# Softmax over 16,384 rows: a schedule written by hand in a critical section, and the same work as a fixed schedule of the tile framework with passes of eight rows

## The chip, the core and the metric

The kernel runs on one core of a Trainium2 chip. Four engines matter here: VectorE (DVE in the profile), ScalarE (ACT), SyncE (SP), which only issues loads and waits, and the core's 16 DMA engines, which carry data between the chip's memory (HBM) and the core's own memory (SBUF, 128 partitions wide). The metric is the device time of one execution in microseconds (us); lower is better.

## What is computed

The input is 32 x 512 rows of 1024 float32 numbers, 64 MiB in all, and the output has the same size. Each row goes through a softmax at temperature 0.5:

```python
scaled = x / temperature
shifted = scaled - np.max(scaled, axis=-1, keepdims=True)
exp_x = np.exp(shifted)
return exp_x / np.sum(exp_x, axis=-1, keepdims=True)
```

Every number is read from HBM once and written once, so 134.2 MB pass through the DMA engines.

## The kernel before

**Tiling.** The 16,384 rows are cut into 16 tiles. A tile has 1024 rows: eight rows in each of the 128 partitions, 4096 KB. A tile is loaded by one DMA and stored by one DMA (`LOADS` and `STORES`). All work is done in place, in a ring in SBUF that has room for 48 rows per partition (`RING`), which is six tiles. A load of tile i therefore has to wait until the store of tile i-6 has landed.

**Passes.** The computing goes in passes of four rows per partition (`GROUP = 4`), two passes to a tile, 32 in all. For pass g there are five steps:

- `maximum(g)` (line 91, VectorE): one reduction finds the largest of each row, for four rows at once.
- `shift(g)` (line 101, VectorE): the maximum times -2 becomes the bias of the exponential.
- `exponential(g)` (line 109, ScalarE): four activations, one for each row, write exp(2x + bias) over the row and sum it up as they go. Each is followed in the profile by a short instruction that reads the accumulator.
- `invert(g)` (line 122, VectorE): the reciprocal of the sums.
- `divide(g)` (line 128, VectorE): four multiplications, one for each row.

**The order of the work.** The whole program stands in one critical section of the framework (`tc.tile_critical()`, line 154), in which the framework inserts nothing: the order on each engine is the order of the code, and every dependence is a semaphore that the code names itself. There are three lists, one for each engine:

- SP issues the 16 loads in order (line 142). From the seventh on it waits for the store that frees the place. After the last load it waits for the remaining stores to land (line 158).
- ScalarE does the exponentials of pass g, and then issues those stores whose last pass is g-1 (`store`, line 149). A store waits for the divisions of its tile. So the store of a tile stands behind four exponentials of the next tile.
- VectorE does maximum and shift of pass g, and then reciprocal and division of pass g-1. So the division of a pass stands behind the maximum of the next pass, and where that pass begins a new tile, behind the wait for that tile's load (line 90).

Loads and stores are issued on two queues, q1 from SP and q10 from ScalarE, and both are served by the same 16 DMA engines. Line 206 of the profile is the end of the framework's context, outside the critical section; it closes every execution.

Of the kernel before, what the change touches and what calls it, by code (L numbers as in the profile page):

```python
# [1 line left out]

# [4 lines left out]

LOADS = [8] * 16  # L10

STORES = [[8]] * 16

RING = 48

GROUP = 4


def _places(loads, ring):
    places, p = [], 0  # L20
    for k in loads:
        if p + k > ring:
            p = 0
        places.append(p)
        p += k
    return places


@with_exitstack
def kernel(  # L30
    ctx: ExitStack,
    tc: tile.TileContext,
    x: bass.AP,
    temperature: bass.AP,
    out: bass.AP,
):
    nc = tc.nc
    f32 = mybir.dt.float32
    scale = 1.0 / float(temperature)
    extreme = mybir.AluOpType.max if scale > 0 else mybir.AluOpType.min  # L40

    P = 128
    xf = x.flatten_outer_dims()
    of = out.flatten_outer_dims()
    n, d = xf.shape
    assert sum(LOADS) * P == n

    places = _places(LOADS, RING)
    first = [sum(LOADS[:i]) for i in range(len(LOADS))]
    total = sum(LOADS)  # L50

    pool = ctx.enter_context(tc.tile_pool(name="data", bufs=1))
    ring = pool.tile([P, RING, d], f32, name="ring")
    top = pool.tile([P, total], f32, name="top")
    bias = pool.tile([P, total], f32, name="bias")
    sums = pool.tile([P, total], f32, name="sums")
    recip = pool.tile([P, total], f32, name="recip")


    parts = []  # L60
    for i, ks in enumerate(STORES):
        j = 0
        for k in ks:
            parts.append((i, places[i] + j, first[i] + j, k))
            j += k
        assert j == LOADS[i]

    groups, part_end = [], []
    for i, s, r, k in parts:
        for a in range(0, k, GROUP):  # L70
            groups.append((i, s + a, r + a, min(GROUP, k - a)))
        part_end.append(len(groups))

    loaded = [tc.alloc_semaphore(f"loaded{i}") for i in range(len(LOADS))]
    stored = [tc.alloc_semaphore(f"stored{i}") for i in range(len(parts))]
    topped, biased, summed, inverted, scaled = (
        tc.alloc_semaphore(name)
        for name in ("topped", "biased", "summed", "inverted", "scaled")
    )

    def dram(t, r, k, i):

        block = t[P * first[i] : P * (first[i] + LOADS[i]), :]
        block = block.rearrange("(p k) d -> p k d", p=P, k=LOADS[i])
        return block[:, r - first[i] : r - first[i] + k, :]

    def maximum(g):
        i, s, r, k = groups[g]
        if g == 0 or groups[g - 1][0] != i:
            nc.vector.wait_ge(loaded[i], 16)  # L90
        nc.vector.tensor_reduce(  # L91
            out=top[:, r : r + k],
            in_=ring[:, s : s + k, :],
            axis=mybir.AxisListType.X,
            op=extreme,
        ).then_inc(topped, 1)

    def shift(g):
        i, s, r, k = groups[g]
        nc.vector.wait_ge(topped, g + 1)  # L100
        nc.vector.tensor_scalar_mul(  # L101
            bias[:, r : r + k], in0=top[:, r : r + k], scalar1=-scale
        ).then_inc(biased, 1)

    def exponential(g):
        i, s, r, k = groups[g]
        nc.scalar.wait_ge(biased, g + 1)
        for a in range(k):
            ins = nc.scalar.activation(  # L109
                ring[:, s + a, :],  # L110
                ring[:, s + a, :],
                mybir.ActivationFunctionType.Exp,
                bias=bias[:, r + a : r + a + 1],
                scale=scale,
                accum_out=sums[:, r + a : r + a + 1],
            )
        ins.then_inc(summed, 1)

    def invert(g):
        i, s, r, k = groups[g]  # L120
        nc.vector.wait_ge(summed, g + 1)
        nc.vector.reciprocal(recip[:, r : r + k], sums[:, r : r + k]).then_inc(inverted, 1)  # L122

    def divide(g):
        i, s, r, k = groups[g]
        nc.vector.wait_ge(inverted, g + 1)
        for a in range(k):
            ins = nc.vector.tensor_scalar_mul(  # L128
                ring[:, s + a, :], in0=ring[:, s + a, :], scalar1=recip[:, r + a : r + a + 1]
            )  # L130
        ins.then_inc(scaled, 1)

    def load(i):
        nonlocal free_to
        s, r, k = places[i], first[i], LOADS[i]

        for n, (l, s1, r1, k1) in enumerate(parts):
            if l < i and s1 < s + k and s < s1 + k1 and n > free_to:
                for b in range(free_to + 1, n + 1):
                    nc.sync.wait_ge(stored[b], 16)  # L140
                free_to = n
        nc.sync.dma_start(out=ring[:, s : s + k, :], in_=dram(xf, r, k, i)).then_inc(
            loaded[i], 16
        )

    def store(n):
        l, s, r, k = parts[n]
        nc.scalar.wait_ge(scaled, part_end[n])
        nc.scalar.dma_start(out=dram(of, r, k, l), in_=ring[:, s : s + k, :]).then_inc(
            stored[n], 16  # L150
        )

    free_to = -1
    with tc.tile_critical():  # L154
        for i in range(len(LOADS)):
            load(i)
        for b in range(free_to + 1, len(parts)):
            nc.sync.wait_ge(stored[b], 16)


        for g in range(len(groups) + 1):
            if g < len(groups):
                exponential(g)
            for n in range(len(parts)):
                if part_end[n] == g:
                    store(n)


        for g in range(len(groups) + 1):
            if g < len(groups):  # L170
                maximum(g)
                shift(g)
            if g > 0:
                invert(g - 1)
                divide(g - 1)


# [1 line left out]
_INS = ['x', 'temperature']  # L179
_OUTS = [((32, 512, 1024), 'float32')]  # L180

_NUMBERS = {'temperature': 0.5}


# [26 lines left out]
```

## Time and profile before

| | us |
|---|---|
| median of 4 runs | 319.08 (318.67 to 319.26) |
| the profiled execution | 318.74 |
| its span, from the first to the last instruction | 317.0 |
| VectorE busy | 235.5 (74%) |
| ScalarE busy | 149.6 (47%) |
| DMA, mean over the span | 424 GB/s |

The span is a little shorter than the time, as the time also holds what lies around the first and the last instruction. Busy shares are means over the whole span. A DMA instruction on a queue only marks the issue; the transfer runs afterwards, and the profile gives the time from the issue to the landing, at which the semaphore has its full count. In lists of stretches, "x" and a number count the instructions that ran in the stretch, and the DMA share is that of all 16 engines; since whole packets are booked to one stretch, a short stretch can read a little over 1 or under it.

### The profile page before, as it was taken

The page shows a single profiled execution, that of the slowest core. Times are in us where ns is not written, and L with a number is a line of the kernel's source. Part 1 is how long each engine was busy: PE and PEld are TensorE (multiplying, and loading weights), DVE is VectorE, ACT ScalarE, POOL GpSimd, SP SyncE. Part 2 cuts the span into 40 slices and gives each one's busy share as a digit, 9 for nine tenths or more (in the row PEclk, how much of TensorE's full clock was granted, in tenths as well). Part 3 has the DMA queues.
Part 4 walks back from the last instruction along what each step waited for, and adds up shares of the span by engine and source line. Part 5 has one row for each costly group of instructions (what it writes and reads, how often), then busy time and mean ns, then how long its engine had stood idle before and what let it go on. Part 6 is the DMA issues. An engine that isn't in the chain of part 4 may idle for free.

```text
span 317.0 us, 568 instructions
## 1 busy us (share of the span) xinstructions
DVE 235.5 (74%) x224; ACT 149.6 (47%) x257; POOL 0.2 (0%) x4
## 2 busy tenths in 40 slices
DVE  0399999999689494995949769496793967949710
ACT  1076666666526255361554606455163551635500
POOL 0000000000000000000000000000000000000000
DMA  8999999999999999999999999999999999999995
GB/s 327 401 463 405 389 455 405 459 420 438 438 426 451 414 447 414 455 418 442 422 438 438 426 451 414 448 414 451 422 438 431 434 442 418 447 418 442 418 447 219
DMA packets 4612, 134.25 MB, mean 424 GB/s; under 512 B 512, under 2 KB 512, under 8 KB 512
## 3 DMA queue, kind: packets, MB, share of 16 engines
q1 hardware_dynamic: 2304, 67.11, 49.5%
q10 hardware_dynamic: 2304, 67.11, 49.0%
q14 instruction: 4, 0.03, 0.0%
HBM read 67.11 MB, written 67.11 MB: 423 GB/s over the span
## 4 chain that ended last, share of the span: by engine, by line
DMA 57%; DVE 29%; ACT 5%; another core or an unknown queue 4%; issue 0%; SPq 0%
DMA ring<-in_x_dram 35%; DMA out_dram<-ring 22%; DVE top L91 18%; DVE ring L128 10%; ACT ring L109 5%; DVE bias L101 1%; DVE recip L122 0%; SPq L206 0%; SPq L154 0%
## 5 line engine op out<-in xcount | busy, mean ns | idle before, releaser
L109 ACT ACTIVATE ring<-ring,bias 128x1024 f32<-128x1024 f32 x128 | 145.4, 1137 | 149.1 <-DVE bias L101 149.1
L91 DVE TENSOR_REDUCE top<-ring 128x4 f32<-128x4096 f32 x32 | 141.3, 4416 | 62.8 <-DMA ring<-in_x_dram 62.8
L128 DVE TENSOR_SCALAR ring<-ring,recip 128x1024 f32<-128x1024 f32 x128 | 87.7, 749 | 1.1
L109 ACT ACTIVATION_READ_ACCUMULATOR ring<-ring,bias 128x1 f32 x128 | 23.9, 186 | 0.0
L122 DVE RECIPROCAL recip<-sums 128x4 f32<-128x4 f32 x32 | 5.5, 171 | 2.0 <-ACT ring L109 2.0
L101 DVE TENSOR_SCALAR bias<-top 128x4 f32<-128x4 f32 x32 | 5.4, 170 | 1.1
L109 ACT ACT_TABLE_LOAD x1 | 1.3, 1283 | 0.9 <-SPq L154 0.9
L192 POOL MEMSET const-bfloat16-1.0<- 128x1 bf16 x1 | 0.1, 102 | 0.0
L192 POOL MEMSET const-uint8-127<- 128x1 uint8 x1 | 0.1, 102 | 0.0
L192 POOL MEMSET const-float32-1.0<- 128x1 f32 x1 | 0.1, 99 | 0.0
L192 POOL MEMSET const-float32-0.0<- 128x1 f32 x1 | 0.1, 98 | 0.2 <-issue 0.2
## 6 DMA issues: line engine op xcount, KB each, us to landing
ring<-in_x_dram SPq DMA_DIRECT2D x16, 4096.0 KB, 49.9
out_dram<-ring ACTq DMA_DIRECT2D x16, 4096.0 KB, 38.9
```

The source lines that it names most:

```text
L91: nc.vector.tensor_reduce(out=top[:, r : r + k], in_=ring[:, s : s + k, :], axis=mybir.AxisListType.X, op=extreme,).then_inc(topped, 1)
L101: nc.vector.tensor_scalar_mul(bias[:, r : r + k], in0=top[:, r : r + k], scalar1=-scale).then_inc(biased, 1)
L109: ins = nc.scalar.activation(ring[:, s + a, :], ring[:, s + a, :], mybir.ActivationFunctionType.Exp, bias=bias[:, r + a : r + a + 1], scal ...
L122: nc.vector.reciprocal(recip[:, r : r + k], sums[:, r : r + k]).then_inc(inverted, 1)
L128: ins = nc.vector.tensor_scalar_mul(ring[:, s + a, :], in0=ring[:, s + a, :], scalar1=recip[:, r + a : r + a + 1])
L192: nc = _bacc.Bacc("TRN2", target_bir_lowering=False, num_devices=1)
```

## The change

The critical section, the ring, the named semaphores and the three separate lists go. In their place stands a fixed schedule of the tile framework (`tc.manual_schedule()`): one list of steps, whose order is kept on each engine, and for which the framework itself puts in the waits. The ring becomes a pool of six tiles (`BUFS = 6`), and the statistics of a pass become four small tiles from a pool of four buffers each. `GROUP` goes from 4 to 8, so a pass is now a whole tile: one reduction over eight rows, one shift, eight activations, one reciprocal and eight multiplications, 16 passes in all.

The list of steps is: six loads; then for each pass g the maximum, the shift and the exponentials of pass g, and after these the reciprocal, the divisions and the store of pass g-1. The load of a further tile is written right after a store. Loads are still issued from SP and stores from ScalarE, in the same sizes, and tiles take the same turns. On VectorE the order is still maximum g before division g-1. On ScalarE a store now stands behind eight exponentials of the next tile, where four stood before.

```diff
-LOADS = [8] * 16
+TILES = [[8]] * 16
+BUFS = 6
-STORES = [[8]] * 16
-RING = 48
-GROUP = 4
+GROUP = 8
...
-    pool = ctx.enter_context(tc.tile_pool(name="data", bufs=1))
-    ring = pool.tile([P, RING, d], f32, name="ring")
-    top = pool.tile([P, total], f32, name="top")
...
+    data = ctx.enter_context(tc.tile_pool(name="data", bufs=BUFS))
+    stats = ctx.enter_context(tc.tile_pool(name="stats", bufs=4))
...
+    def load():
+        i = len(tiles)
+        if i < len(TILES):
+            xt = data.tile([P, sum(TILES[i]), d], f32, name="xt")
+            nc.sync.dma_start(out=xt, in_=dram(xf, i))
+            tiles.append(xt)

     def maximum(g):
-        i, s, r, k = groups[g]
-        if g == 0 or groups[g - 1][0] != i:
-            nc.vector.wait_ge(loaded[i], 16)
+        i, a, k, _ = groups[g]
+        top, bias, sums, recip = (
+            stats.tile([P, k], f32, name=name) for name in ("top", "bias", "sums", "recip")
+        )
+        small.append((bias, sums, recip))
         nc.vector.tensor_reduce(
-            out=top[:, r : r + k],
-            in_=ring[:, s : s + k, :],
-            axis=mybir.AxisListType.X,
-            op=extreme,
-        ).then_inc(topped, 1)
+            out=top, in_=tiles[i][:, a : a + k, :], axis=mybir.AxisListType.X, op=extreme
+        )
+        nc.vector.tensor_scalar_mul(bias, in0=top, scalar1=-scale)
...
     def divide(g):
-        i, s, r, k = groups[g]
-        nc.vector.wait_ge(inverted, g + 1)
+        i, a, k, _ = groups[g]
+        _, sums, recip = small[g]
+        nc.vector.reciprocal(recip, sums)
...
+    def store(g):
+        i, _, _, part = groups[g]
+        if part:
+            a, k = part
+            nc.scalar.dma_start(out=dram(of, i)[:, a : a + k, :], in_=tiles[i][:, a : a + k, :])
+            if a + k == sum(TILES[i]):
+                load()
...
-    with tc.tile_critical():
-        for i in range(len(LOADS)):
-            load(i)
...
+    with tc.manual_schedule():
+        for _ in range(BUFS):
+            load()
         for g in range(len(groups) + 1):
             if g < len(groups):
                 maximum(g)
-                shift(g)
+                exponential(g)
             if g > 0:
-                invert(g - 1)
                 divide(g - 1)
+                store(g - 1)
```

More of the change, by code (lines that the diff above doesn't have):

```diff
@@ L6 @@
 from concourse._compat import with_exitstack
-LOADS = [8] * 16
-STORES = [[8]] * 16
-RING = 48
-GROUP = 4
[L19 to L26, printed above, removed]
+TILES = [[8]] * 16
+BUFS = 6
+GROUP = 8
 @with_exitstack
@@ L45 @@
     n, d = xf.shape
[L46 to L50, printed above, removed]
-    pool = ctx.enter_context(tc.tile_pool(name="data", bufs=1))
-    ring = pool.tile([P, RING, d], f32, name="ring")
-    top = pool.tile([P, total], f32, name="top")
[L55 to L60, printed above, removed]
@@ L61 @@
-    for i, ks in enumerate(STORES):
-        j = 0
-        for k in ks:
[L64 to L85, printed above, removed]
-    def maximum(g):
-        i, s, r, k = groups[g]
-        if g == 0 or groups[g - 1][0] != i:
-            nc.vector.wait_ge(loaded[i], 16)
-        nc.vector.tensor_reduce(
-            out=top[:, r : r + k],
-            in_=ring[:, s : s + k, :],
-            axis=mybir.AxisListType.X,
-            op=extreme,
-        ).then_inc(topped, 1)
@@ L98, in shift @@
-    def shift(g):
-        i, s, r, k = groups[g]
[L100 to L103, printed above, removed]
-    def exponential(g):
[L106 to L111, printed above, removed]
+    assert sum(sum(ks) for ks in TILES) * P == n
@@ new lines, with dram @@
+    data = ctx.enter_context(tc.tile_pool(name="data", bufs=BUFS))
+    stats = ctx.enter_context(tc.tile_pool(name="stats", bufs=4))
+    groups, first, r = [], [], 0
+    for i, ks in enumerate(TILES):
+        first.append(r)
+        r += sum(ks)
+        a = 0
+        for k in ks:
+            for b in range(0, k, GROUP):
+                m = min(GROUP, k - b)
+                groups.append((i, a + b, m, (a, k) if b + m == k else None))
+            a += k
+    def dram(t, i):
+        k = sum(TILES[i])
+        block = t[P * first[i] : P * (first[i] + k), :]
+        return block.rearrange("(p k) d -> p k d", p=P, k=k)
@@ new lines @@
+    tiles, small = [], []
+    def load():
[4 more added lines that the diff above has]
+            tiles.append(xt)
+    def maximum(g):
+        i, a, k, _ = groups[g]
[3 more added lines that the diff above has]
+        small.append((bias, sums, recip))
+        nc.vector.tensor_reduce(
+            out=top, in_=tiles[i][:, a : a + k, :], axis=mybir.AxisListType.X, op=extreme
+        )
+        nc.vector.tensor_scalar_mul(bias, in0=top, scalar1=-scale)
@@ L112, in exponential @@
+    def exponential(g):
+        i, a, k, _ = groups[g]
+        bias, sums, _ = small[g]
+        for b in range(k):
+            nc.scalar.activation(
+                tiles[i][:, a + b, :],
+                tiles[i][:, a + b, :],
                 mybir.ActivationFunctionType.Exp,
-                bias=bias[:, r + a : r + a + 1],
+                bias=bias[:, b : b + 1],
                 scale=scale,
-                accum_out=sums[:, r + a : r + a + 1],
+                accum_out=sums[:, b : b + 1],
@@ L116, in exponential @@
             )
[L117 to L122, printed above, removed]
-    def divide(g):
-        i, s, r, k = groups[g]
-        nc.vector.wait_ge(inverted, g + 1)
-        for a in range(k):
-            ins = nc.vector.tensor_scalar_mul(
-                ring[:, s + a, :], in0=ring[:, s + a, :], scalar1=recip[:, r + a : r + a + 1]
-            )
-        ins.then_inc(scaled, 1)
@@ L133, in load @@
[L133 to L151, printed above, removed]
@@ L153 @@
-    free_to = -1
-    with tc.tile_critical():
-        for i in range(len(LOADS)):
-            load(i)
[L157 to L166, printed above, removed]
+    def divide(g):
+        i, a, k, _ = groups[g]
+        _, sums, recip = small[g]
+        nc.vector.reciprocal(recip, sums)
+        for b in range(k):
+            nc.vector.tensor_scalar_mul(
+                tiles[i][:, a + b, :], in0=tiles[i][:, a + b, :], scalar1=recip[:, b : b + 1]
+            )
```

## The prediction

> **What bounds the kernel now.** I read the page's slices first, then its queues and its chain, then the busy time stretch by stretch through the tail, then the order of events there. Whole page first:
>
> ```profile
> DMA  8999999999999999999999999999999999999995
> q1 hardware_dynamic: 2304, 67.11, 49.5%
> q10 hardware_dynamic: 2304, 67.11, 49.0%
> DMA 57%; DVE 29%; ACT 5%; another core or an unknown queue 4%; issue 0%; SPq 0%
> L91 DVE TENSOR_REDUCE top<-ring 128x4 f32<-128x4096 f32 x32 | 141.3, 4416 | 62.8 <-DMA ring<-in_x_dram 62.8
> ring<-in_x_dram SPq DMA_DIRECT2D x16, 4096.0 KB, 49.9
> out_dram<-ring ACTq DMA_DIRECT2D x16, 4096.0 KB, 38.9
> ```
>
> The 16 DMA engines are busy in every slice but the first and the last; loads (q1) take 49.5% of the span and stores (q10) 49.0%. VectorE idles 62.8 us, all of it for loads. A load takes 49.9 us from issue to landing and a store 38.9, though one load and one store together need only 19.36 us of the engines (below): both queues hold work well ahead. The chain's 29% VectorE is therefore work under a busy DMA, not the bound.
>
> The busy time by stretch, at both ends (columns: DVE, ACT, POOL, clock, DMA share, GB/s):
>
> ```profile
> 0.00:1.90 1.90, 0.00 (x0) 1.00 (x1) 0.20 (x4) 1.00 0.00 0
> 5.00:33.00 28.00, 19.43 (x17) 12.10 (x21) 0.00 (x0) 1.00 1.01 438
> 240.00:280.00 40.00, 29.46 (x28) 19.01 (x33) 0.00 (x0) 1.00 1.00 433
> 294.00:302.60 8.60, 6.62 (x12) 4.64 (x8) 0.00 (x0) 1.00 1.03 446
> 303.60:306.00 2.40, 0.00 (x0) 0.00 (x0) 0.00 (x0) 1.00 0.98 423
> 306.00:313.00 7.00, 0.00 (x0) 0.00 (x0) 0.00 (x0) 1.00 1.01 435
> 313.00:313.50 0.50, 0.00 (x0) 0.00 (x0) 0.00 (x0) 1.00 0.16 66
> ```
>
> Loads alone move 438 GB/s, loads with stores 433, stores alone 435: the mix does not matter, and no stretch is left idle up to about 313.3. Bytes do not change, so the end can move only by a hole in the DMA, or at the two edges outside 1.9 to 313.3 us.
>
> Now the tail in order of time:
>
> ```profile
> 282.90 4.42 DVE L91 TENSOR_REDUCE top<-ring 128x4 f32<-128x4096 f32 x1 [4.48 <-DMA ring<-in_x_dram]
> 290.41 0.34 ACTq L149 DMA_DIRECT2D out_dram<-ring  x1
> 290.88 0.19 ACT L109 ACTIVATION_READ_ACCUMULATOR ring<-ring,bias 128x1 f32 x1
> 290.97 1.13 ACT L109 ACTIVATE ring<-ring,bias 128x1024 f32<-128x1024 f32 x1
> 292.01 0.19 ACT L109 ACTIVATION_READ_ACCUMULATOR ring<-ring,bias 128x1 f32 x1
> 299.83 2.74 DVE L128 TENSOR_SCALAR ring<-ring,recip 128x1024 f32<-128x1024 f32 x4
> 302.60 0.34 ACTq L149 DMA_DIRECT2D out_dram<-ring  x1
> ```
>
> The last load (tile 15) has landed at 282.88; the load before it started a maximum at 263.55 in the chain, so a load and a store together take 19.36 us of the DMA, one transfer 9.68. From the end back, store 15 had its slot from 303.6 to 313.3 and store 14 from 293.9. Store 14 was issued 3.5 us ahead of its slot, store 15 only 1.0 us ahead, and no hole is seen at 303.6. So the tail has no slack to spare: that is what the change must be tried against.
>
> **The change, part by part.** Times are those of the profiled execution (317.0 us of span, 318.74 us in all, 1.74 us around the span). It lies 0.34 us under the median of 319.08.
>
> *Maximum over eight rows.* 32 maxima of 4.416 us become 16. From 141.3 us, halved, each is at most 8.83; by the rate of 4096 elements and the short gap between two (4.42 us pitch) I take 8.7. Shift and reciprocal halve from 32 to 16 each: (5.4 + 5.5)/2 = 5.5 us of VectorE saved. It lies in the 62.8 us that VectorE waits for loads, so 0.
>
> *Exponential and division over eight rows.* Same instructions, later pass. Four exponentials took 4.64 us in the chain; eight take 9.2. Eight divisions by the 0.66 us at which they follow one another take 5.4 (four took 2.74). What moves is when a store can go: division of tile i now waits behind the maximum of the whole of tile i+1, where before only half of it stood in front. In the tail: load i+1 lands, 0.02, maximum 8.68, bias and reciprocal 0.32, division 5.39, 0.03 to the issue: 14.4 us, where 290.41 - 282.88 = 7.5 was before. Each store is 6.9 us later against the next load's landing.
>
> *What pays in the middle.* Nothing, as long as the queues hold work. VectorE needs 8.7 + 0.3 + 5.4 = 14.4 us a tile against 19.36 of DMA. A store lands 38.9 us after its issue where 19.36 would do, so about 19 us of lead stands against the delay; loads have 49.9 - 19.36 = 30 us of it. On SP each load stays queued behind the landing of the store of six tiles before, as now (lines 137 to 142 before, the pool's release after). The loads have that lead, so a store that lands 7 us later leaves no hole.
>
> *The first store.* It decides when loads stop having the DMA alone. Before: issued at 32.92. After: load 0 lands at 13.19 and its maximum and bias end at 22.1; load 1 lands at 13.19 + 9.68 = 22.9. Then the same 14.4 us: 37.3. Loads have 4.4 us more alone, and what they gain there they need not share later. Loads and stores halve the rate, so the last load lands 4.4 us earlier: 282.88 - 4.4 = 278.5.
>
> *The tail then.* Store 14 is issued at 278.5 + 14.4 = 292.9, its slot opens at 293.9: a lead of 1.0 us, the same that store 15 had before without a hole. The length of the passes falls out of this: a longer pass delays the first store, brings the last load forward and delays store 14 by equal amounts. Store 15 follows exponential (278.5 + 8.9 + 9.2 = 296.6), reciprocal 0.2 and division 5.4: issued at 302.2, before its slot at 303.6. Hole 0; bounds 0 and 1.6 (a lead of 1.0 was enough at 302.6; but the first load of all took 12.25 us from issue to landing, 2.6 over its 9.68, and if all of that lay ahead of the data a lead of 1.0 falls 1.6 short). I take 0, from the nearer row, also a store behind a store.
>
> *The store's place on ScalarE.* Store g-1 stands behind all eight exponentials of pass g. At 290.41 the store went out 0.03 us after the division's end with three ScalarE instructions before it not yet begun (290.88, 290.97, 292.01): ScalarE's queue runs at least that far ahead. With eight rows, at the division's end about 4.8 rows have run and seven instructions are left. If only three may be left, each store goes 1.3 us later, the first too: last load at 277.2, store 14 again at 292.9, store 15 at 300.9. Cost 0 to 0.
>
> [...]
>
> [...]
>
> *No critical section.* Start: the chain has the section's steps on SP from 0.71 to 0.94 ahead of the first load; 0 to 0.23 saved, I take 0.1. End: the last store lands 12.87 us after its issue, at 315.47, and the framework's own end (line 206) starts on SP at 316.0 and lasts to 317.0. Between lies the section's release (line 154), 0.5 us. The whole-context end stays. 0 to 0.5 saved, and I take 0.4, since the remaining waits for landed stores stay on SP. Should the framework add a second handshake of that length, 0.95 is lost instead. Waits that it adds to single instructions fall on VectorE, ScalarE and SP, which have the leads above; without these, a wait for each of the 16 maxima, reciprocals and stores at the chain's usual 0.02 us of issue would cost 1 us.
>
> Sum: 318.74 - 0.1 - 0.4 + 0 = 318.24 against the profiled execution; against the median 319.08 - 0.5 = 318.6.
>
> **The rivals.**
> - *The head start is not kept (slower).* If loads are held by the ring rather than the DMA, the last load still lands at 282.88, store 14 goes out at 297.3 and the DMA is empty from 293.9 to 298.3: 4.4 us, 323.0. SP's waits for stores (225.1 us in ten waits) speak for it; the 30 us of lead of each load against. It decides once the last load lands later than 278.5, us for us. 7%.
> - *The lead of 1.0 us is too short.* Up to 1.6 us of hole before store 14: 318.6 + 1.6 = 320.2 at most. For it: the first load; against: store 15 before. 13%.
> - *The edges give more.* 0.23 and 0.5, and a shorter clearing of semaphores (0.27 now) as fewer are named: 1.0 us, 318.1. 12%.
> - *The framework costs more than the section.* Its added handshake or waits: 319.08 + 0.95 = 320.0. 8%.
> - *Nothing of it is felt.* The DMA is full and the edges are alike: 319.1. 5%.
>
> **How the numbers follow.** Forecast as argued: 55%, with 317.9 to 319.0 by the edges' bounds and 0.3 us of scatter (the four runs lie between 318.67 and 319.26). About 0.2%, 0.64 us, is what a measurement here can tell from no change; the forecast's gain of 0.5 lies under it, and with that scatter I give it 22 of the 55 beyond and 33 within. Edges: 12 faster. Short lead: 9 within, 4 slower. Nothing felt: 5 within. Head start lost 7 and framework 8: slower. Together 0.34 faster, 0.47 same, 0.19 slower. The range runs from 317.9 to 320.0: it leaves out the lost head start and the ends of the others.
>
> **What would show it.** DMA share of 1.0 through to 313; the first store issued at 37 to 39 us; the last load landed at 277 to 279; stores 14 and 15 issued near 292.9 and 301 to 302; VectorE's wait for loads larger by some 5 us; the span's end 1.0 us after the last landing. Wrong would be a hole after the last load, a first store that comes late with the last load not earlier, or a wait of SP or ScalarE on something that is not named above.

## The result, and the profile after

The changed kernel takes 317.89 us in the median of 43 runs (317.27 to 319.98, and one run at 324.06 that stands apart and is left out of the ratio); the kernel before, beside it, 318.83 us in 64 runs (318.60 to 319.48). The ratio is 0.9978, with a 95% interval from 0.9970 to 0.9986: about 0.7 us faster, on the border of what can be told. More telling than the median is the spread. The kernel before keeps within 0.9 us. Of the changed kernel's other 42 runs, 32 lie from 317.27 to 318.52, and ten from 319.18 to 319.98, all above the median of the kernel before. The profiled execution, with 319.47 us, is one of these ten, which is lucky for the reading: it shows what happens in one of them.

The page of the changed kernel, the lines that answer to those of before, and the queue that fetches instructions:

```profile
DMA  8999999999999999999999999999999999999994
...
q1 hardware_dynamic: 2304, 67.11, 49.4%
q10 hardware_dynamic: 2304, 67.11, 49.1%
q14 instruction: 3, 0.02, 0.0%
...
L70 DVE TENSOR_REDUCE top<-xt 128x8 f32<-128x8192 f32 x16 | 139.0, 8685 | 67.6 <-DMA xt<-in_x_dram 67.6
```

The DMA is as full as before, and VectorE waits 4.8 us more for loads, as forecast. Instruction fetches on q14 are three, where the page of before has four. The tail in order of time:

```profile
273.27 0.34 ACTq L101 DMA_DIRECT2D out_dram<-xt  x1
273.38 0.19 ACT L79 ACTIVATION_READ_ACCUMULATOR xt<-xt,bias 128x1 f32 x1
...
276.77 0.19 ACT L79 ACTIVATION_READ_ACCUMULATOR xt<-xt,bias 128x1 f32 x1
278.18 8.69 DVE L70 TENSOR_REDUCE top<-xt 128x8 f32<-128x8192 f32 x1 [4.94 <-DMA xt<-in_x_dram]
...
292.64 0.34 ACTq L101 DMA_DIRECT2D out_dram<-xt  x1
...
302.01 0.34 ACTq L101 DMA_DIRECT2D out_dram<-xt  x1
```

The last load is in at 278.2 (before: 282.9), store 14 goes out at 292.6 and store 15 at 302.0. No hole follows. But the end is ragged, as the busy time by stretch shows (columns as in the prediction):

```profile
302.00:312.50 10.50, 0.00 (x0) 0.00 (x0) 0.00 (x0) 1.00 1.01 437
312.50:313.50 1.00, 0.00 (x0) 0.00 (x0) 0.00 (x0) 1.00 0.54 229
313.50:315.00 1.50, 0.00 (x0) 0.00 (x0) 0.00 (x0) 1.00 0.20 87
315.00:317.80 2.80, 0.00 (x0) 0.00 (x0) 0.00 (x0) 1.00 0.11 47
```

Here a few engines still work after 315. Before, hardly anything was started after 313.5:

```profile
313.50:314.00 0.50, 0.00 (x0) 0.00 (x0) 0.00 (x0) 1.00 0.16 66
314.00:315.20 1.20, 0.00 (x0) 0.00 (x0) 0.00 (x0) 1.00 0.00 0
```

The two edges, from the chain's start and from the line at which the framework's context ends:

```profile
0.73 0.36 SPq L61
```

```profile
L147 SPq DRAIN  x3: 7/7/7, 317.0 to 317.3; - x3
...
L147 POOLq EVENT_SEMAPHORE_RANGE_CLEAR  x1: 93/93/93, 317.3 to 317.3; - x1
```

The same places before:

```profile
0.94 57.23 SPq L142 DMA_DIRECT2D ring<-in_x_dram  x7
```

```profile
L206 SPq DRAIN  x3: 7/7/7, 316.0 to 316.3; - x3
...
L206 POOLq EVENT_SEMAPHORE_RANGE_CLEAR  x1: 265/265/265, 316.4 to 316.4; - x1
```

The first load is issued at 0.73 in place of 0.94. The last store is issued at 302.01 and lands after 14.86 us, at 316.88; the span ends 0.9 us later. Before, 1.5 us lay between 315.47 and 317.0. So the edges give 0.2 + 0.6 = 0.8 us, and in this execution the ragged end, landing 1.4 us later than before (316.88 against 315.47), takes more than that back: 317.8 us of span against 317.0.

To see which engine ends late, I read the trace packet by packet. In the profiles of before and of the changed kernel an engine's next packet starts 4 ns after the end of the one before (median), so packets of 32 KB can be strung into 16 rows, each packet to the one that starts where it ends. A packet takes 1.213 us in the median of both. The table has one profile of each kernel, most of the experiments below among them (times in us; the median engine is the eighth of the 16 to end):

```
                            time of   first packet of store 2,  store packets over     median    last      fetches of
kernel                      this run  from the nearest load's   1.25 us, at 45-100 us  engine's  engine's  the last
                                                                                       end       end       engine
before                      318.74     7.7 us                     1 of 354           313.5    315.1   2
changed                     319.47    -1.4                       56 of 354           313.5    316.5   0
changed, again              317.65    -1.0                       27 of 352           313.5    314.7   0
section, eight              318.53    -1.2                       20 of 352           313.8    314.5   2
four, in step               318.11    -0.4                        0 of 354           313.6    315.1   2
four                        318.16     7.3                        0 of 352           313.4    315.1   2
head delayed                317.57     6.0                        0 of 368           313.2    314.3   2
head delayed, again         317.66     6.6                        0 of 368           313.4    314.4   2
more instructions           317.79     5.8                        0 of 368           313.3    314.8   2
head and tail delayed       317.76    -4.8                        0 of 345           313.0    314.7   2
two stores later            317.41    -6.1                        0 of 342           313.3    314.5   2
```

Two things stand in it that the prediction did not have. First, the median engine ends at nearly the same time in every kernel (313.0 to 313.8); the end of the program is that of the slowest engine, and before that was an engine that had also fetched instructions twice (at 65 and 240 us, 0.31 us each). Second, in the changed kernel four engines that fetched next to nothing end 3 us late: in their packets of stores between 45 and 100 us, many took 1.25 to 1.75 us. What these packets took beyond 1.213 us adds up to 9.4 us, some 2.3 us for each of four engines, so it is most of the 3 us. In the changed kernel profiled again it adds up to 4.5 us and in the section with eight rows to 2.9 us, and there the last engine ends 1.2 and 0.7 us after the median one. Of these three profiles only the first is of one of the long runs, so one execution alone shows what makes a run long.

In the changed kernel store k starts its packets at the same time as load k+4, within 1.4 us. In the kernel before it starts 7.7 us after one. From here on "in step" means the former.

### The profile page after: what moved, and what is told of

Read it like the earlier page. It is cut to its first block, busy times and chain, and to the rows that moved or that the text cites. A ratio compares the mean times of both kernels' runs of the same rounds, so it can differ in the third digit from the quotient of the medians.

```text
span 317.8 us, 558 instructions
## 1 busy us (share of the span) xinstructions
DVE 229.5 (72%) x176; ACT 147.9 (47%) x257; POOL 0.2 (0%) x4
## 4 chain that ended last, share of the span: by engine, by line
DMA 59%; DVE 28%; ACT 6%; another core or an unknown queue 1%; issue 1%; DVEq 0%; SPq 0%; ACTq 0%
DMA xt<-in_x_dram 31%; DMA out_dram<-xt 28%; DVE top L70 19%; DVE xt L93 8%; ACT xt L79 6%; DVE bias L73 0%; DVE recip L91 0%; DVEq L147 0%; SPq L61 0%; ACTq L101 0%; ACTq L79 0%
## 5 line engine op out<-in xcount | busy, mean ns | idle before, releaser
L79 ACT ACTIVATE xt<-xt,bias 128x1024 f32<-128x1024 f32 x128 | 145.1, 1135 | 135.4 <-DVE bias L73 130.1
L70 DVE TENSOR_REDUCE top<-xt 128x8 f32<-128x8192 f32 x16 | 139.0, 8685 | 67.6 <-DMA xt<-in_x_dram 67.6
L93 DVE TENSOR_SCALAR xt<-xt,recip 128x1024 f32<-128x1024 f32 x128 | 86.3, 749 | 0.6
L79 ACT ACTIVATION_READ_ACCUMULATOR xt<-xt,bias 128x1 f32 x128 | 23.9, 187 | 0.0
L91 DVE RECIPROCAL recip<-sums 128x8 f32<-128x8 f32 x16 | 3.1, 195 | 3.7 <-ACT xt L79 3.7
L73 DVE TENSOR_SCALAR bias<-top 128x8 f32<-128x8 f32 x16 | 2.7, 171 | 0.6
```

What stands on the lines that cost most here:

```text
L70: nc.vector.tensor_reduce(out=top, in_=tiles[i][:, a : a + k, :], axis=mybir.AxisListType.X, op=extreme)
L73: nc.vector.tensor_scalar_mul(bias, in0=top, scalar1=-scale)
L79: nc.scalar.activation(tiles[i][:, a + b, :], tiles[i][:, a + b, :], mybir.ActivationFunctionType.Exp, bias=bias[:, b : b + 1], scale=scal ...
L91: nc.vector.reciprocal(recip, sums)
L93: nc.vector.tensor_scalar_mul(tiles[i][:, a + b, :], in0=tiles[i][:, a + b, :], scalar1=recip[:, b : b + 1])
```

## The experiments

The medians below belong to different chips, so ratios are against the runs of the kernel before on the same chip.

| kernel | median us (range) | runs | ratio (95%) |
|---|---|---|---|
| framework, four rows | 318.05 (317.80 to 318.45) | 11 | 0.9975 (0.9967 to 0.9984) |
| section, eight rows | 319.11 (318.53 to 320.60) | 12 | 1.0017 (1.0003 to 1.0031) |
| changed, head delayed | 317.62 (317.55 to 317.81) | 5 | 0.9965 (0.9953 to 0.9976) |
| the same again | 317.55 (317.38 to 317.74) | 5 | 0.9957 (0.9945 to 0.9969) |
| changed, tail delayed | 323.99 (323.66 to 324.28) | 4 | 1.0163 (1.0148 to 1.0177) |
| changed, both delayed | 317.76 (317.69 to 317.82) | 5 | 0.9962 (0.9949 to 0.9975) |
| four rows in step | 319.01 (317.99 to 320.80) | 12 | 1.0007 (0.9987 to 1.0026) |
| more instructions | 317.99 (317.54 to 318.12) | 5 | 0.9967 (0.9955 to 0.9979) |
| changed again | 318.52 (317.28 to 319.89) | 12 | 0.9993 (0.9975 to 1.0011) |
| two stores later | 317.31 (317.24 to 317.41) | 5 | 0.9950 (0.9937 to 0.9962) |

### Each part of the change alone

The framework's schedule with passes of four rows:

```diff
-GROUP = 8
+GROUP = 4
```

> The framework's schedule alone, passes of four rows as before. Theory 'edges' (the gain is the critical section's own steps at both ends, 0.21 us at the start and 0.58 us after the last landing between the two profiles, whatever the passes): median 317.4 to 318.1, some 0.8 us under the kernel before. Theory 'passes' (the gain comes from half as many VectorE instructions): 318.8, as before. Theory 'step' (the runs of the changed kernel that take 319.2 to 320.0 are those in which store k runs in step with load k+4, because the first store starts as load 4 starts, and four DMA engines then take 1.3 to 1.5 us for a store's packet in place of 1.21): here the first store starts near 37 us, half a tile away from the loads, so no run above 318.6.

It came to 318.05, with no run above 318.45. "Edges" and "step" hold, "passes" does not: 0.25% is gained (0.16 to 0.33%) with the passes as they were. The first store goes out at 32.68, out of step.

The critical section of the kernel before with passes of eight:

```diff
-GROUP = 4
+GROUP = 8
```

> The critical section kept, passes of eight rows. 'Edges': 318.8, as before, since both ends keep the section's steps. 'Passes': 317.9, like the changed kernel. 'Step': the first store starts near 41.8 us, in step with load 4, so part of the runs lies 1.5 to 2 us above the rest, over 320, and the median is 318.8 or a little above.

It came to 319.11. Six of twelve runs lie between 318.53 and 318.70, where the kernel before has its lowest, and six between 319.51 and 320.60. Passes of eight bring no gain by themselves; they bring the spread, with the section too. So the change is a gain of its first half and a risk from its second.

### The tail's lead and the head's delay

The prediction rests on a balance: a first store that goes later lets the loads run ahead, and what the tail loses the head has given. An added maximum of VectorE, whose result nobody uses, delays one division:

```diff
+EXTRA = {0: 4}        # pass: rows; {14: 8} and {0: 8, 14: 8} in the others
...
+    def again(g):
+        i, a, _, _ = groups[g]
+        k = EXTRA.get(g, 0)
+        if k:
+            waste = stats.tile([P, k], f32, name="waste")
+            nc.vector.tensor_reduce(
+                out=waste, in_=tiles[i][:, a : a + k, :], axis=mybir.AxisListType.X, op=extreme
+            )
...
             if g > 0:
+                again(g - 1)
                 divide(g - 1)
```

At the head:

> The changed kernel with one more maximum over four rows of tile 0 (4.3 us of VectorE, result unused) ahead of the first division. The full-DMA theory: the first store goes 4.3 us later (41.5), the last load lands 4.3 us earlier (273.8), and the time is unchanged, 317.4 to 318.0, although 4.3 us of work was added. A rival in which each delay of a store is paid: 322. 'Step': the first store starts half a tile away from load 4, so no run above 318.6; without 'step' a quarter of the runs lies at 319.2 to 320.0 as in the changed kernel.

4.4 us of work was added and the time did not rise: it came to 317.62. The first store went out at 41.45, the last load was in at 273.2. At the tail:

> The changed kernel with one more maximum over eight rows of tile 14 (8.6 us of VectorE, result unused) ahead of the division of tile 14, the last store but one. If that store has a lead of about 1 us only, as predicted, the DMA is empty for 8.6 - 0.7 = 7.9 us after store 13, store 14 is issued at 301.3, and the time is 325.5 to 326.5. If the tail had slack: 318.

It came to 323.99, 6.4 us above the kernel with the head delayed. The busy time by stretch, and the issue that ends the hole, which the list merges with that of store 15 at 305.9:

```profile
293.00:294.00 1.00, 1.00 (x1) 1.00 (x3) 0.00 (x0) 1.00 0.76 328
294.00:295.00 1.00, 0.96 (x3) 1.00 (x3) 0.00 (x0) 1.00 0.01 0
295.00:300.30 5.30, 5.30 (x9) 0.43 (x2) 0.00 (x0) 1.00 0.00 0
300.30:301.10 0.80, 0.77 (x3) 0.00 (x0) 0.00 (x0) 1.00 0.00 0
301.10:302.00 0.90, 0.90 (x3) 0.00 (x0) 0.00 (x0) 1.00 1.35 583
```

```profile
300.34 5.88 ACTq L112 DMA_DIRECT2D out_dram<-xt  x2
```

The DMA stands still from 294 to 301.2, and the first packet starts 0.84 us after the issue. So there is a hole, and it is paid. It was priced at 7.9, and two things make the price smaller: the last load is in at 277.3 and not at 278.5, so that store 14 leaves earlier; and after the hole all 16 engines start together and end within 0.2 us of one another, so the ragged end of some 1 us is gone. With both delays:

> The changed kernel with both delays of 8.6 us: one more maximum over eight rows ahead of the division of tile 0 and one ahead of the division of tile 14 (results unused). The full-DMA theory, in which the first store's delay brings the last load forward by as much: first store issued at 45.8, last load landed at 269.5 or so, store 14 issued near 292, the DMA without a hole, time 317.5 to 318.0, although the tail's delay alone took 323.99. A rival in which the tail's delay is paid whatever the head does: 323 to 324. 'Step': stores run about half a tile away from the loads, so no run above 318.6.

```profile
45.69 0.37 ACTq L112 DMA_DIRECT2D out_dram<-xt  x1
...
268.48 8.69 DVE L72 TENSOR_REDUCE top<-xt 128x8 f32<-128x8192 f32 x1 [4.95 <-DMA xt<-in_x_dram]
...
291.52 5.88 ACTq L112 DMA_DIRECT2D out_dram<-xt  x2
```

The same delay that cost 6.4 us in the tail costs nothing, 317.76, once the first store is as late as well: the last load is in 8.8 us earlier than with the tail's delay alone (268.5 against 277.3), and store 14 is back at 291.5. This shows the balance on which the prediction rests.

### Step

The kernel with the head delayed was out of step and had no run above 317.81. It was run again for more of them:

> The same kernel as with the first store delayed by 4.3 us (317.62, from 317.55 to 317.81 in 5 runs), for more runs on the same chip as the others: 317.4 to 317.9, none above 318.6 by 'step', and 0.25 to 0.5 us under passes of four without delay.

317.38 to 317.74. And the reverse, passes of four, put into step by the same added maximum:

```diff
-GROUP = 8
+GROUP = 4
+EXTRA = {1: 4}        # the second pass of tile 0
```

> Passes of four rows in the framework's schedule, with one more maximum over four rows ahead of the second division of tile 0, so that the first store is issued near 37.1 us, as with passes of eight, and runs in step with load 4. 'Step': the runs spread as those of the changed kernel do, a quarter or more of them 1 to 2 us above the lowest, which stays at 317.8 to 318.0; the median is 318.0 to 319. If instead the pass of eight itself spreads them (longer reductions, other turns of VectorE and ScalarE): all within 317.8 to 318.5, as with passes of four without the delay (318.05).

It came to 319.01, from 317.99 to 320.80; seven of twelve runs lie above 318.6, against none of eleven without the delay. The size of the pass is not what spreads the runs; the moment of the first store is. The changed kernel itself, without an edit, was run beside the next one:

> The changed kernel itself, on the same chip as the kernel with the shifted output, to have its spread beside it: lowest 317.3 to 317.6, a quarter to a half of the runs over 318.6, up to 321.

Six of twelve lie from 317.28 to 317.74 and six from 319.30 to 319.89. Taken together: in step, three kernels have an upper group of runs, apart from the lower one by a gap of 0.57 us or more (10 of 42 and 6 of 12 of the changed kernel, 6 of 12 with the section, 7 of 12 with four rows). Out of step, in six experiments with 36 runs, there is none. The kernel with the tail delayed is in step as well (its store 2 starts 1.0 us ahead of a load), and its four runs lie within 0.62 us. They are few, and after their DMA's standstill from 294 to 301.2 us all 16 engines start together, so they say little either way.

Slack in the tail is not what decides. With four rows in the framework's schedule, store 15 is issued at 302.66, 0.9 us ahead of its slot, and there is no upper group. Put into step, the same kernel issues it at 297.46, 6.1 us ahead, and has one.

What the step does was tried by moving the output alone:

```diff
+HALF = 512
...
-            nc.scalar.dma_start(out=dram(of, i)[:, a : a + k, :], in_=tiles[i][:, a : a + k, :])
+            lo = P * first[i] + HALF
+            if i < len(TILES) - 1:
+                block = of[lo : lo + P * k, :].rearrange("(p k) d -> p k d", p=P, k=k)
+                nc.scalar.dma_start(out=block, in_=tiles[i])
+            else:
+                for b, p in ((of[lo : lo + HALF, :], 0), (of[0:HALF, :], P // 2)):
+                    b = b.rearrange("(p k) d -> p k d", p=P // 2, k=k)
+                    nc.scalar.dma_start(out=b, in_=tiles[i][p : p + P // 2, :, :])
```

> The changed kernel in step, but every tile is stored 512 rows (2 MB, half a tile) further on in the output, the last half tile going to its beginning as a second DMA: the output is the reference's rolled by 512 rows. Times, queues and partitions stay as they are; only the distance in HBM between what is read and what is written at the same moment changes by 2 MB. If step hurts by HBM addresses: the spread vanishes, all runs 317.3 to 318.6. If it hurts on the side of SBUF (load and store in the same partition at the same moment) or by the engines' turns alone: 25% or more of the runs at 319 to 321, as in the changed kernel. The second DMA of the tail may add up to 0.5 us to all.

It came to 325.67 (325.31 to 326.63) and settles nothing, since its last two stores spoil it: each over 64 partitions and 2048 KB, they moved 186 to 268 GB/s together from 306 to 318 us, where the stores of the kernel before, over 128 partitions, moved 435 from 306 to 313 us. In its profile two of 355 store packets between 45 and 100 us are over 1.25 us. The second attempt has one DMA at the end:

```diff
+HALF = 512
...
+            lo = P * first[i] + HALF
+            m = k if i < len(TILES) - 1 else k // 2
+            block = of[lo : lo + P * m, :].rearrange("(p k) d -> p k d", p=P, k=m)
+            nc.scalar.dma_start(out=block, in_=tiles[i][:, 0:m, :])
```

> Once more the changed kernel, in step, with every tile stored 512 rows (2 MB) further on, now without a second DMA: of the last tile only four of eight rows a partition are stored, and the first 512 rows of the output are not written, so that 2 MB less is moved, at 431 GB/s 4.9 us less. If step hurts by HBM addresses: all runs within 0.6 us near 312.7. If it hurts in SBUF or by the engines' turns alone: the lowest near 312.5, a quarter or more of the runs 1 to 2.5 us above.

It stores only half of the last tile and leaves the first 512 rows of the output unwritten. It came to 312.72, from 312.55 to 312.99 in five runs, ratio 0.9807 (0.9794 to 0.9820) with 2 MB less moved. No packet of 358 is over 1.25 us, though store 2 starts within 0.4 us of a load. That fits a cost that hangs on the distance in HBM between what is read and what is written at the same moment, and not on the partitions or on the turns of the queues, which stayed. It is not shown. Of the changed kernel's runs a half (6 of 12) to three quarters (32 of 42) were undisturbed, so five undisturbed ones in a row come by chance in 3 to 26% of cases. The packets do not settle it either: four rows in step, without any shift, had none of 354 over 1.25 us in its profile. Whether it is HBM at all, and what in it, why only a few of the 16 engines suffer, and why an execution in step can also go without, stay open.

### Instructions

72 small instructions in the kernel with the head delayed, run on `idle`, a tile of eight numbers a partition:

```diff
+SMALL = 6
...
+    idle = stats.tile([P, 8], f32, name="idle")
...
+        nc.vector.memset(idle, 1.0)
...
+                if 1 < g < 14:
+                    for _ in range(SMALL):
+                        nc.vector.tensor_scalar_mul(idle, in0=idle, scalar1=1.0)
```

> The kernel with the delayed first store (passes of eight, 317.62) with 72 more small VectorE instructions over 12 passes, at times when VectorE waits for loads. Theory 'fetch' (the 0.4 us between passes of four, 318.05, and of eight off step, 317.62, is the fetching of instructions on q14, which takes turns on the DMA engines: the engine that fetched most ends last): 4 or 5 fetches in place of 3 and a median of 317.8 to 318.1. Otherwise 317.6.

Four fetches and 317.99, against 317.55 on the same chip without them, and the last engine, again one with two fetches, ends at 314.8 and not 314.4. The median is where "fetch" puts it, but the ranges overlap (317.54 to 318.12 and 317.38 to 317.74), and the profile of the kernel with both delays also has four fetches at 317.76. It speaks for "fetch", at some 0.2 to 0.4 us, without closing it.

### A version that beats both

The delay needs no added work. The division and store of tile 0 can go behind the maximum and the exponentials of tile 2:

```diff
-            if g > 0:
-                divide(g - 1)
-                store(g - 1)
+            for h in [] if g < 2 else [0, 1] if g == 2 else [g - 1]:
+                divide(h)
+                store(h)
```

> The changed kernel, with the division and the store of tile 0 moved behind the maximum and the exponentials of tile 2; no added work. First store issued near 47, in place of 37.2, about half a tile out of step, last load landed near 268. By the full-DMA theory and 'step': 317.4 to 317.8, none above 318.6, 1.2 us under the kernel before. Without 'step': the changed kernel's spread, up to 320.

```profile
46.90 0.38 ACTq L101 DMA_DIRECT2D out_dram<-xt  x1
...
269.65 8.69 DVE L70 TENSOR_REDUCE top<-xt 128x8 f32<-128x8192 f32 x1 [4.93 <-DMA xt<-in_x_dram]
...
284.10 0.34 ACTq L101 DMA_DIRECT2D out_dram<-xt  x1
...
293.48 0.34 ACTq L101 DMA_DIRECT2D out_dram<-xt  x1
```

317.31, from 317.24 to 317.41: 0.5% under the kernel before (0.38 to 0.63%); about half of that, 0.25%, is the framework's schedule alone. The runs lie within 0.17 us, and only those with both delays are closer together (0.13 us). Its last store waits in the queue for some 10 us before its slot at 303.4; the tail has slack again.

## Why the prediction was right, and where it was off

**The direction and the range.** 318.6 was forecast, from 317.9 to 320.0, and 317.89 was measured, at the range's lower bound. By medians 0.94 us were gained and by the ratio 0.7, where 0.5 was forecast. Both lie above the 0.64 us that the prediction held to be just measurable, but the interval of the ratio, 0.45 to 0.96 us, holds it, and the chances of faster (0.34) and same (0.47) were close to each other.

Part of this is luck. Two misses pull opposite ways: the edges gave 0.3 us more than forecast, and the spread, which was not foreseen, lengthens some runs by 1.5 to 2.5 us. A median hides the second as long as it strikes fewer than half of the runs. When the same kernel was run again and half were struck, the median was 318.52 and the ratio 0.9993. The lower bound of 317.9 is also lower than the terms named beside it give: 319.08 less the edges' 0.73 and 0.3 of scatter is 318.05.

**A full DMA.** Right. Share 1.0 through to 312.5, the same transfers, no hole in the tail. VectorE's halved instructions gained nothing on its own path, as costed.

**The balance of head and tail.** Right, in mechanism and nearly in size: first store at 37.2 (37.3 forecast), last load at 278.2, and at 277.1 when the kernel was profiled again (278.5), store 14 at 292.6 and 291.6 (292.9), store 15 at 302.0 and 301.0 (302.2). The lead of store 14 was larger than the 1.0 us it was given: the slot opened at 294.3 and 293.9, so 1.7 and 2.3 us. The rival of the lost head start (323.0) is refuted by these times, and the one of the short lead by the 0.84 us that store 14 needed when the tail was delayed.

**ScalarE's queue.** The forecast's 37.3 us for the first store lets all seven instructions that are left stand ahead of it, which no run had shown at that time: the row of before shows three. In the changed kernel the store at 273.27 leaves with seven ScalarE instructions ahead of it not begun (273.38 to 276.77), so the three were a lower bound, and the case of stores that go 1.3 us later did not come. By the forecast's sums either gives the same end; only the one was run.

**The start of a transfer.** With the tail delayed, store 14 found the DMA idle and its first packet started 0.84 us after the start of the issue at 300.34. That is less than the 1.0 us of the opening before (issue at 0.94, nothing moved until 1.9), and far less than the 2.6 us on which the bound of 1.6 rests.

**No critical section: the term that was mis-sized.** 0.1 + 0.4 was taken, 0.2 + 0.6 measured. The start gave nearly all of its bound of 0.23. At the end, the section's release (0.5) went as a whole, and the framework's own clearing of semaphores fell from 0.27 to 0.09 us, which only the rival "the edges give more" had counted. The framework's schedule alone is 0.25% faster, 0.8 us, and confirms the size. Of the five rivals this one came nearest.

**The step that failed: "the mix does not matter".** Loads with stores were priced at one rate whatever runs beside what, because the stretches of before showed 438, 433 and 435 GB/s. In the kernel before, stores ran 7.7 us out of step. The prediction moved the first store by 4.4 us and asked only what that does to the order of the work; it also put stores into step with loads, which costs 1.5 to 2.5 us in a quarter to a half of the changed kernel's executions. Without this the changed kernel would take what it takes in its better runs: 317.6 in their median, from 317.3 to 318.5. Why being in step costs this much, and why only in some executions, stays open.

## What to carry to other kernels

With the DMA full from end to end, engines' work counted here only through the first store and the last stores: a delay in every pass cancelled (store 14 left 14.5 us after the last load in place of 7.5, and the median engine ended at 313.5 as before), a delay in the tail alone was paid (6.4 us for one of 8.7), and delaying the first store bought slack for the tail (with both delays nothing was paid, 317.76). Price a framework's entry and exit by reading the trace before the first transfer and after the last landing; it was the whole gain here. And where loads and stores of equal size stream side by side, look at their distance in time, and perhaps in address: here a shift of the first store by some 4 to 10 us took the spread out of the runs and made the kernel 0.3 to 0.5% faster than before, of which the framework's schedule alone gives 0.25%.

## What was not expected of the hardware

- Stores in step with loads that lie a whole number of tiles of 4 MB away had up to 56 of 354 packets at 1.25 to 1.75 us in place of 1.213, on a few of the engines, between 45 and 100 us, in some executions and not in others. With 2 MB between, 2 of 355 and none of 358 had in two profiles, but without it one profile in step also had none of 354.
- The stream ended with its slowest engine: in the eleven profiles of the table the last of 16 ended 0.7 to 3.0 us after the median one. In nine of them it was an engine that had fetched instructions twice; a fetch took 0.3 us, and the packet after it 0.1 to 0.6 us more than others.
- Two DMAs over 64 partitions each, in flight together, moved 186 to 268 GB/s; the last stores of the kernel before, over 128 partitions, 435.
- The first store behind six queued loads started its packets 4.4 us (before) and 4.6 us (changed) after its issue, and 3.7 to 4.9 us over all runs; a store with the DMA idle started them 0.84 us after.
